# A two-layer encoder whose MLP runs by seven block products: activation sums move into the up product, weight sums move to VectorE, and the first two groups go product by product

## The chip, the cores and the metric

The kernel runs on one core of one Trainium2 chip. The metric is device time: microseconds from start to end of one execution, as a median over runs. The profile is one further execution, recorded by the hardware profiler.

## The reference

What is computed is a trunk of two layers on 1024 tokens of 1024 features in fp32. Each layer adds an attention part and an MLP to x; a last norm follows. The change touches the MLP alone, whose hidden width is 4096:

```python
for l in range(DEPTH):                       # DEPTH = 2
    ...                                      # four kinds of attention heads
    x = x + mix @ w_out[l]
    h = rms_norm(x, norm2_g[l])
    x = x + jnp.square(jax.nn.relu(h @ w_up[l])) @ w_down[l]
return rms_norm(x, final_norm_g)
```

`rms_norm` divides each token's row by the root of its mean square and multiplies by a gain per feature.

## The kernel before

**Data.** x lies in SBUF as eight tiles of 128 features by 1024 tokens, and every product is transposed: features on partitions, tokens along the row. The trace names the tiles x_7209, x_7244, x_7279, x_7314 (features 0 to 511, tiles 0 to 3) and x_6860, x_6927, x_6987, x_7073 (tiles 4 to 7, which the output projection finishes first).

**A matmul is three.** TensorE multiplies fp32 numbers as pairs of fp32r numbers, a high and a low half, in three passes: high weights by high rows (L211), high weights by low rows (L212), low weights by high rows (L213). So each operand has to be split first. The high half is a copy that ScalarE casts (L186), the low half what is left after the high half is subtracted (L180; L190 where the norm's gain is multiplied in). For activations VectorE makes the low half. For weights GpSimd makes it: `wh` is ScalarE's, `wl` GpSimd's, and each has three buffers. All element-wise two-operand work, sums and low halves alike, goes through the helper `tt`, which is L180 on whatever engine.

**Seven products.** Each of the MLP's two products is done in 2 x 2 blocks by seven block products instead of eight, with sums of activations and sums of weights as operands. For the up product the tokens are cut into two halves (n = 0, 1), the input features into two halves (tiles 0 to 3 and 4 to 7), and the hidden features into pairs of output tiles q and q + 16. A **group** is one such q; there are 16. It loads four weight tiles of 128 x 512, called 11, 12, 21 and 22, sums them into further ones (s1 = 21 + 22, and three subtractions in `combos`, on VectorE, all in tiles called `raw`), and runs seven products on TensorE. A product of a group is a **block** of 12 matmuls of 128 x 512: four tiles of input features by three passes. The seven **operands** of activations, 1 to 7, are the same for all groups: operand 1 is the first token half of features 0 to 511, times the gain, 2 the same of features 512 to 1023, 3 the second token half of features 512 to 1023, and 4 to 7 are differences and sums of these. Each is four pairs of high and low tiles, `near` for operands 1, 2 and 6, `far` for the others. **Product n** is the block with operand n, or by its weights: 11 by operand 1, 12 by operand 2, the 21 sum by 7, 22 by 4, s1 by 5, the 11 sum by 6, the 12 sum by 3.

**From PSUM to DRAM.** The four results of a group (two output tiles by two token halves) come out of PSUM over VectorE (L180 with a PSUM tile u, p or q) and ScalarE (copies at L1218, L1228, L1232). Then VectorE multiplies the positive part by `rb` (L1199), the norm's factor of each token, copied to all partitions. ScalarE squares it (L1201), and it is stored to a DRAM array, `acts`, all four stores issued by SyncE. `rb` is made in the opening: ScalarE squares the eight x tiles, VectorE adds them up (tiles `sq`, 128 x 1024), TensorE sums over partitions (L252), VectorE takes the inverse root (L238 to L242, `rs_r`), TensorE spreads it over all partitions (L288), and VectorE copies it out of PSUM (L283). The text calls the last two the **spread of the norm's rows**.

**The down product.** `acts` is read back 128 x 512 at a time (`act`). The hidden features are cut into four **quarters**, each with seven products of four blocks: 28 blocks a quarter, 112 a layer, the same number as in the up product. Each quarter loads 16 weight tiles and 16 activation tiles. It makes the sums of weights on GpSimd (`raw<-raw`, 16 a quarter) and the sums of activations on VectorE (`act<-act`, 16 a quarter), splits the operands into tiles called `op`, and adds each block's result into x on VectorE as it leaves PSUM (`x<-u`, `x<-p`). After the last quarter of layer 1 the final norm runs for each half of the tokens: `final(0)` stands ahead of the last eight blocks, `final(1)` behind them.

**Stages.** The text cuts each MLP into four stretches: the **opening** (from the last eviction of the output projection to the first product), the **up body** (the 112 blocks of the up product), the **hand-over** (the first 16 blocks of the down product) and the **rest of the down product**.

**What sets the order.** TensorE's order in the MLP is written out by hand (`manual_schedule`): the program's own order. The other engines' order is set by a scheduler that goes by an estimate of times, with priorities by place in the program. Loads and stores stand in SyncE's queue in its order. Before the change all seven operands are made ahead of the first product. Buffers come from pools that open and close: `up` with `prep` for the opening and then `ev` for the results inside it, and `down` after all of them are closed. Two more pools outlive these: one of 16 tiles of 128 x 1024 (`big`, of which `far` and `op` are made) and the weight halves'.

## Time and profile before

| what | value |
|---|---|
| median of 3 runs | 3167.83 us |
| lowest, highest | 3164.23, 3170.88 us |
| the profiled execution | 3169.88 us |
| its span (first to last instruction) | 3168.1 us |
| mean granted TensorE clock | 0.900 |
| before the first MLP's opening | 0 to 848.85 us |
| first MLP | 848.85 to 1572.40 us: 723.55 |
| layer 1 ahead of its MLP's opening | 1572.40 to 2413.65 us: 841.25 |
| second MLP and final norm | 2413.65 to 3168.10 us: 754.45 |

The span is from the first to the last instruction of the profiled execution; the time of an execution holds 1.8 us more. PE is TensorE's matmuls, PEld its weight loads, DVE VectorE, ACT ScalarE, POOL GpSimd, SP SyncE. An arrow `out<-in` gives an instruction's tiles. In a row of waits or of idle time, what stands behind `<-` is what ended it. The granted clock is a share of full speed. Line numbers are those of the kernel before.

### The profile page before, as it was taken

Reading aid. Unit: us, or ns where it says so; the run is one execution under the profiler, and the core shown is the slowest. Engines: PE = TensorE matmul, PEld = TensorE weight load, DVE = VectorE, ACT = ScalarE, POOL = GpSimd, SP = SyncE. Lnnn points to the kernel's source line nnn. Section 1 sums busy time; section 2 is a strip of 40 time slices with the busy share of each in tenths; the row PEclk is TensorE's granted clock in tenths of the full one; section 3 lists DMA queues with packets and bytes.
Section 4 is the critical chain, followed back from the end, with each engine's and each line's share of the span. In section 5 each row is a group of like instructions: output and inputs, shape, how many; then the busy total and the mean of one; then the engine's idle time right before and its main releaser. Section 6 shows DMA issues by size and latency. Waiting matters only on the chain.

```text
span 3168.1 us, 36820 instructions
## 1 busy us (share of the span) xinstructions
PE 2697.7 (85%) x12310; PEld 2168.3 (68%) x12310; DVE 1970.6 (62%) x3402; ACT 1430.8 (45%) x2525; POOL 1334.0 (42%) x882
## 2 busy tenths in 40 slices
PE   8579996999779996999976789868995999969997
PEld 6357864677568884777864678646884788747775
DVE  6376843576554447888554767446757444488885
ACT  4256743555344443343414567335644444334344
POOL 2254541210224445788523446211111444468882
PEclk9689986799889998999986899868997999979998
DMA  4322464421223324332232225643211233253311
GB/s 161 111 86 94 137 199 144 142 74 58 65 64 107 113 94 153 113 97 83 82 101 92 84 103 160 194 151 100 81 63 43 90 107 112 85 193 96 96 45 53
DMA packets 159045, 334.59 MB, mean 106 GB/s; under 512 B 17848, under 2 KB 24968, under 8 KB 158856
## 3 DMA queue, kind: packets, MB, share of 16 engines
q1 hardware_dynamic: 158856, 332.25, 32.5%
q8 instruction: 97, 1.59, 0.2%
q14 instruction: 92, 0.75, 0.1%
HBM read 233.93 MB, written 98.25 MB: 105 GB/s over the span
## 4 chain that ended last, share of the span: by engine, by line
PE 59%; DMA 16%; DVE 11%; issue 5%; POOL 4%; ACT 2%; SPq 2%; POOLq 0%; DVEq 0%; ACTq 0%
PE u L213 7%; PE u L211 7%; PE u L212 7%; PE mm L211 4%; PE mm L212 4%; PE mm L213 4%; PE p L213 3%; PE p L211 3%; PE p L212 3%; PE sb L778 3%; DMA ws<-in_w_in 3%; PE tr L814 2%; POOL wl L180 2%; POOL raw L180 2%; DMA kb<-both 2%
## 5 line engine op out<-in xcount | busy, mean ns | idle before, releaser
L180 POOL TENSOR_TENSOR wl<-raw,wh 128x512 fp32r<-128x512 f32 x448 | 632.9, 1415 | 637.7 <-ACT wh L186 626.5
L186 ACT ACTIVATE wh<-raw 128x512 fp32r<-128x512 f32 x448 | 280.9, 627 | 583.4 <-PE u L212 306.8
L180 POOL TENSOR_TENSOR wl<-ws,wh 128x512 fp32r<-128x512 f32 (+1 forms) x114 | 149.7, 1316 | 611.6 <-ACT wh L186 581.1
L180 DVE TENSOR_TENSOR op<-act,op 128x512 fp32r<-128x512 f32 x224 | 291.3, 1333 | 31.7 <-ACT op L186 31.5
L180 DVE TENSOR_TENSOR ptl<-tr,pth 128x512 fp32r<-128x512 f32 (+2 forms) x384 | 238.4, 629 | 114.5 <-ACT pth L186 112.8
L186 ACT ACTIVATE pth<-tr 128x512 fp32r<-128x512 f32 (+2 forms) x384 | 205.7, 547 | 184.6 <-PE tr L814 102.4
L783 ACT ACTIVATE p<-p,nm 128x1024 f32<-128x1024 f32 x192 | 219.9, 1146 | 88.9 <-DVE nm L780 85.3
L211 PE MATMUL u<-op,wh 128*128 128x512 f32 x512 | 209.1, 408 | 59.3 <-ACT wh L186 38.0
L778 PE MATMUL sb<-stack 96*128 96x512 f32 x640 | 219.5, 426 | 29.2 <-DVE nm L780 27.8
L180 POOL TENSOR_TENSOR p<-p 128x1024 f32<-128x1024 f32 x64 | 153.3, 2399 | 183.5 <-ACT p L867 167.4
L213 PE MATMUL u<-op,wl 128*128 128x512 f32 x512 | 210.0, 410 | 18.4 <-POOL wl L180 18.2
L180 DVE TENSOR_TENSOR raw<-raw 128x512 f32<-128x512 f32 x128 | 91.0, 714 | 196.0 <-POOL wl L180 167.0
L180 POOL TENSOR_TENSOR raw<-raw 128x512 f32<-128x512 f32 x128 | 212.4, 1671 | 0.5
L212 PE MATMUL u<-op,wh 128*128 128x512 f32 x512 | 208.0, 406 | 1.2 <-DVE op L180 1.0
L211 PE MATMUL mm<-xh,wh 128*128 128x512 f32 x416 | 175.2, 421 | 29.0 <-ACT wh L186 27.6
L186 ACT ACTIVATE op<-act 128x512 fp32r<-128x512 f32 x224 | 139.5, 629 | 90.7 <-DVE act L180 63.5
L802 PE MATMUL pv<-pth,v 128*128 128x256 f32 x512 | 150.2, 307 | 29.6 <-ACT pth L186 16.4
L212 PE MATMUL mm<-xl,wh 128*128 128x512 f32 x416 | 171.4, 412 | 0.0
L213 PE MATMUL mm<-xh,wl 128*128 128x512 f32 x416 | 170.4, 410 | 0.3
L780 DVE CUSTOM_DVE_ANT_0 p<-sb,zero,nm 128x512 f32<-128x512 f32 x192 | 142.5, 743 | 42.7 <-PE sb L778 39.6
L814 PE MATMUL tr<-ident,p 128*128 128x128 f32 x1024 | 161.3, 277 | 3.9 <-DVE ptl L180 2.8
L186 ACT ACTIVATE wh<-ws 128x512 fp32r<-128x512 f32 (+1 forms) x114 | 69.5, 611 | 202.3 <-PE mm L212 93.4
(245 smaller groups left out, 7143.6 us busy)
## 6 DMA issues: line engine op xcount, KB each, us to landing
raw<-in_w_up SPq DMA_DIRECT2D x128, 256.0 KB
raw<-in_w_down SPq DMA_DIRECT2D x128, 256.0 KB
act<-acts SPq DMA_DIRECT2D x128, 256.0 KB
ws<-in_w_in SPq DMA_DIRECT2D x76, 256.0 KB
acts<-u SPq DMA_DIRECT2D x64, 256.0 KB
rz<-drows SPq DMA_DIRECT2D x40, 256.0 KB
acts<-p SPq DMA_DIRECT2D x32, 256.0 KB
acts<-c SPq DMA_DIRECT2D x32, 256.0 KB
```

Of the source, the lines that this page charges most:

```text
L180: (eng or self.nc.vector).tensor_tensor(out=out, in0=a, in1=b, op=op)
L186: nc.scalar.activation(hi, src, AF.Copy)
L211: mm(ps, w[0], x[0][:, sl], start=start, stop=False)
L212: mm(ps, w[0], x[1][:, sl], start=False, stop=False)
L213: mm(ps, w[1], x[0][:, sl], start=False, stop=stop)
L778: self.nc.tensor.matmul(ps, q[:, qt * P:(qt + 1) * P], k[:, sl], start=i == 0, stop=i == len(passes) - 1)
L780: self.nc.vector.tensor_tensor_reduce(out=p[:, sl], in0=ps, in1=self.zero[:, 0:1].bitcast(F).broadcast_to([P, 512]), scale=-scale, scalar= ...
L783: self.nc.scalar.activation(p, p, AF.Exp, bias=nm[:, 1:2], scale=-1.0, accum_out=z)
L802: nc.tensor.matmul(out, v[:, kt], h[:, sl], start=kt == 0, stop=False)
L814: nc.tensor.transpose(t[:, k * 256 + i * P:k * 256 + (i + 1) * P], p[:, (j * 2 + k) * P:(j * 2 + k + 1) * P], self.ident)
```

## The change

**In the up product.** Each group now stores all seven operands that the down product needs instead of four results: `acts` gets the shape [16, 8, 128, 512], operand o of group q in `acts[q, o]`. Three of these (1, 2, 3) are squared results, and their stores are issued by ScalarE, right behind the squares. The other four (5, 6, 7, 4) are differences that VectorE makes in the up product (`t1`, `t2`, `u2`, `n4`, tiles `ev<-ev`), four instructions a group; SyncE issues their stores. In the first two groups the blocks go product by product: as soon as an operand is there, its product runs for both groups, in the order 2, 1, 6, 5, then 7, 4, 3. The norm's squares come in two parts, tiles 4 to 7 ahead of operand 1 in the program, and the spread of the norm's rows stands between product 5 and product 7. From group 2 on product 12 precedes product 11, and products 4 and 3 of a group run during the next group, as before. A weight tile of 12 is loaded first.

**In the down product.** Quarters go 0 to 3, and each takes the groups 4j to 4j + 3 and weights j and j + 4. All seven operands are loaded (28 tiles a quarter for 16), and no sum of activations is made. The 16 sums of weights a quarter go from GpSimd to VectorE, three of the four behind product 12's blocks, the last behind product 7's. The first weights and operand of the first quarter are given a higher priority by 300 places (`AHEAD`), so that the scheduler may put them ahead of the end of the up product. The order of products within a quarter is 1, 2, 6, 7, 4, 5, 3, as before, and `final(0)` moves behind product 5's four blocks, ahead of product 3's.

**Pools.** One pool serves both products of a layer: 24 tiles of 128 x 512 called `near` (operands 1, 2 and 6 of the up product, then the down product's raw weights), 10 called `raw` (the up product's weights, then the activations read back) and 9 called `ev` (results on their way to `acts`; also the final norm's squares). `t`, `v`, `sq` and `far` are tiles of the `big` pool.

**Numbers.** Per layer GpSimd has 64 instructions less and VectorE 64 more in weight sums; the activation sums, 64 a layer, change their place on VectorE; 48 stores and 48 loads of 256 KB are added.

The diff's core:

```diff
@@ -1111,19 +1111,30 @@
-        acts = self.dram.tile([32, P, S], F, tag="acts", bufs=1, name="acts")
-        with tc.manual_schedule(engines={mybir.EngineType.PE}):
-            self.mlp_up(l, acts)
-            self.mlp_down(l, acts)
+        acts = self.dram.tile([16, 8, P, 512], F, tag="acts", bufs=1, name="acts")
+        with tc.manual_schedule(engines={mybir.EngineType.PE}), \
+                tc.tile_pool(name=f"mlp{l}", bufs=1, reuse_waits="tile") as mp:
+            self.mlp_up(l, acts, mp)
+            self.mlp_down(l, acts, mp)
+    def piece(mp, tag, dt=F, name=None):
+        return mp.tile([P, 512], dt, tag=tag, bufs={"near": 24, "raw": 10, "ev": 9}[tag], name=name or tag)
...
@@ mlp_up @@
+            def relu2(v, src, n):
+                nc.vector.scalar_tensor_tensor(out=v, in0=src, scalar=0.0, in1=rb[:, N[n]],
+                                               op0=ALU.max, op1=ALU.mult)
+                nc.scalar.activation(v, v, AF.Square)
+                return v
+            def keep(q, o, v, eng=None):
+                (eng or nc.scalar).dma_start(acts[q, o], v)
...
+            def p4(s):
+                self.block(s.u, s.c["22"], ops[4], start=False)
+                s.b21 = relu2(tmp(), s.u, 0)
+                keep(s.q, 2, s.b21)
+                self.tt(s.u3, s.p, s.u3, ALU.add)
+                relu2(s.u3, s.u3, 1)
+                keep(s.q, 3, s.u3)
+            def p3(s):
+                self.block(s.p, s.c["12"], ops[3], start=False)
+                self.tt(s.u2, s.p, s.u2, ALU.add)
+                relu2(s.u2, s.u2, 1)
+                t1, t2, n4 = tmp(), tmp(), tmp()
+                sub(t1, s.u2, s.p1)
+                keep(s.q, 5, t1, nc.sync)
+                sub(t2, s.u3, t1)
+                keep(s.q, 6, t2, nc.sync)
+                sub(s.u2, s.u3, s.u2)
+                keep(s.q, 7, s.u2, nc.sync)
+                sub(n4, s.b21, t2)
+                keep(s.q, 4, n4, nc.sync)
...
+            first = [group(q) for q in range(2)]
+            ops[2] = [self.rows_split(near(), x(k + 4, 0), gk(k + 4)) for k in range(4)]
+            for s in first:
+                p12(s)
+            acc = self.squares(self.x[4:], self.big, "big", 16)
+            ops[1] = [self.rows_split(near(), x(k, 0), gk(k)) for k in range(4)]
+            for s in first:
+                p11(s)
...
+            ops[6] = [self.rows_split(near(), t[k]) for k in range(4)]
+            for s in first:
+                p6(s)
+            for s in first:
+                p5(s)
+            acc = self.squares(self.x[:4], self.big, "big", 16, acc)
+            self.spread_here(rb, self.rstd_cols(acc, DM, self.ones[:, 0:1]))
...
@@ mlp_down @@
-            for i, j in enumerate((0, 2, 1, 3)):
-                w = lambda m, h: self.raw_weights(mp, d["w_down"][l, m, 2 * j + h], 20)
...
-                    self.tt(s1[m], a21[m], a22[m], ALU.add, nc.gpsimd)
-                    self.tt(a21[m], a11[m], a21[m], ALU.subtract, nc.gpsimd)
-                    self.tt(a11[m], s1[m], a11[m], ALU.subtract, nc.gpsimd)
-                    self.tt(a12[m], a12[m], a11[m], ALU.subtract, nc.gpsimd)
-                for k in range(4):
-                    sub(b11[k], b12[k], b11[k])
...
+                with tc.high_priority(offset=0 if j else self.AHEAD):
+                    a11, t = [w(m, 0) for m in M], raw_op(1)
+                b = [self.rows_split(self.far(), v) for v in t]
+                for m in M:
+                    self.block(u[m], a11[m], b)
                     add(m, 0, u[m])
...
+                for m in M:
+                    ps = self.bank("p")
+                    self.block(ps, a12[m], b)
+                    add(m, 0, ps)
+                    s1.append(self.raw_weights(mp, "near"))
+                    self.tt(s1[m], a21[m], a22[m], ALU.add)
+                    sub(a21[m], a11[m], a21[m])
+                    sub(a11[m], s1[m], a11[m])
...
```

How the instructions stand is shown at three places of layer 0. First VectorE in the opening, before the change, from x's last evictions (`x_7314<-mm,sum`) on. `t` are the differences on which operands 5, 6 and 4 rest, `near` the low halves of operand 1 (x_7209 to x_7314) and operand 2 (x_6860 on).

```order
L180 TENSOR_TENSOR x_7314<-mm,sum 128x512 x2
L180 TENSOR_TENSOR t<-x_7209 128x512
L180 TENSOR_TENSOR t<-x_7244 128x512
L180 TENSOR_TENSOR t<-x_7279 128x512
L180 TENSOR_TENSOR t<-x_7314 128x512
L190 SCALAR_TENSOR_TENSOR near<-x_7209,par,near 128x512
L190 SCALAR_TENSOR_TENSOR near<-x_7244,par,near 128x512
L190 SCALAR_TENSOR_TENSOR near<-x_7279,par,near 128x512
L190 SCALAR_TENSOR_TENSOR near<-x_7314,par,near 128x512
L190 SCALAR_TENSOR_TENSOR near<-x_6860,par,near 128x512
```

Here operand 1 is followed by operand 2. After the change, where `opl` and `oph` are the low and high halves that were called `near`, `far<-t,far` are low halves of operand 5, `t<-x,par,t` are the sums for operand 6, and L181, L191 and L1251 are what L180, L190 and L1176 were:

```order
L181 TENSOR_TENSOR x_7314<-mm,sum 128x512
L1251 SCALAR_TENSOR_TENSOR t<-x_6987,par,t 128x512
L181 TENSOR_TENSOR t<-x_7314 128x512
L191 SCALAR_TENSOR_TENSOR opl<-x_6860,par,oph 128x512
L191 SCALAR_TENSOR_TENSOR opl<-x_6927,par,oph 128x512
L191 SCALAR_TENSOR_TENSOR opl<-x_6987,par,oph 128x512
L181 TENSOR_TENSOR far<-t,far 128x512
L181 TENSOR_TENSOR raw<-raw 128x512
L1251 SCALAR_TENSOR_TENSOR t<-x_7073,par,t 128x512
L181 TENSOR_TENSOR sq<-sq 128x1024
```

The low halves of operand 2 now come first, three of the four subtractions into `t` stand ahead of x's last eviction, and sums for operand 6, low halves of operand 5, weight sums (`raw<-raw`) of the first two groups and the norm's sums (`sq<-sq`) stand between the low halves that the first products need.

Next VectorE in the hand-over, before the change: the last results of group 15 (u_9862, c_9914, u_9861), then the down product's operands (`op<-act,op`) and its first sums into x.

```order
L180 TENSOR_TENSOR u_9862<-p,u_9862 128x512
L1199 SCALAR_TENSOR_TENSOR u_9862<-u_9862,rb 128x512
L1199 SCALAR_TENSOR_TENSOR c_9914<-u,rb 128x512
L180 TENSOR_TENSOR u_9861<-p,u_9861 128x512
L1199 SCALAR_TENSOR_TENSOR u_9861<-u_9861,rb 128x512
L180 TENSOR_TENSOR op<-act,op 128x512 x4
L180 TENSOR_TENSOR x_7209<-u,x_7209 128x512
L180 TENSOR_TENSOR op<-act,op 128x512
L180 TENSOR_TENSOR x_7244<-u,x_7244 128x512
```

After the change, at the same place (`ev` are the results of groups 14 and 15, `far<-act,far` the down product's operands, `raw<-raw` its weight sums):

```order
L181 TENSOR_TENSOR far<-act,far 128x512
L181 TENSOR_TENSOR raw<-raw 128x512
L1181 SCALAR_TENSOR_TENSOR ev<-u,rb 128x512
L1181 SCALAR_TENSOR_TENSOR ev<-ev,rb 128x512
L181 TENSOR_TENSOR far<-act,far 128x512 x2
L181 TENSOR_TENSOR raw<-raw 128x512
L181 TENSOR_TENSOR far<-act,far 128x512 x2
L181 TENSOR_TENSOR ev<-p,ev 128x512
L181 TENSOR_TENSOR far<-act,far 128x512
L181 TENSOR_TENSOR raw<-raw 128x512
L181 TENSOR_TENSOR far<-act,far 128x512
L1181 SCALAR_TENSOR_TENSOR ev<-ev,rb 128x512
```

The low halves of the down product's operands and its weight sums, of which none stood ahead of group 15's results on VectorE before, are now mixed with these.

Last, ScalarE in the up body, before the change: the casts of weights (`wh<-raw`), the copies out of PSUM and the squares of one group.

```order
L1228 ACTIVATE u_8661<-u 128x512
L186 ACTIVATE wh<-raw 128x512 x2
L1232 ACTIVATE u_8662<-u 128x512
L186 ACTIVATE wh<-raw 128x512
L1201 ACTIVATE u_8662<-u_8662 128x512
L1218 ACTIVATE p_8709<-u 128x512
L186 ACTIVATE wh<-raw 128x512
L1201 ACTIVATE p_8709<-p_8709 128x512
L186 ACTIVATE wh<-raw 128x512
```

After the change, where L1183 is the square, L1208, L1217 and L1198 are the copies and L1187 is the issue of a store:

```order
L1208 ACTIVATE ev<-u 128x512
L187 ACTIVATE wh<-raw 128x512 x2
L1217 ACTIVATE ev<-u 128x512
L187 ACTIVATE wh<-raw 128x512
L1183 ACTIVATE ev<-ev 128x512
L1187 DMA acts<-ev 128x512
L187 ACTIVATE wh<-raw 128x512
L1198 ACTIVATE ev<-u 128x512
L187 ACTIVATE wh<-raw 128x512
```

The issue of a store now stands behind a square in ScalarE's queue, ahead of the next cast of weights; there are three a group.

272 lines of the change are left out of this document (135 added, 137 removed).

## The prediction

> **What bounds the kernel now.** I read the page first: its span and busy times.
>
> ```profile
> span 3168.1 us, 36820 instructions
> PE 2697.7 (85%) x12310; PEld 2168.3 (68%) x12310; DVE 1970.6 (62%) x3402; ACT 1430.8 (45%) x2525; POOL 1334.0 (42%) x882
> ```
>
> TensorE is busy 85% of the time and no other engine comes near, so the question is where the other 15% lies. The two MLPs, cut at TensorE's own edges, answer it for the part that the change touches. The columns are the stretch, its length, the busy time of PE, PEld, DVE, ACT and POOL, the granted clock, the DMA share and GB/s. The rows are opening, up product, hand-over (to the 16th down block) and rest of the down product, for layer 0 and then for layer 1.
>
> ```profile
> 848.75:898.43 49.68, 7.12 (x34) 6.92 (x33) 45.75 (x70) 28.01 (x42) 6.58 (x3) 0.53 0.14 42
> 898.43:1204.50 306.07, 305.38 (x1346) 252.35 (x1345) 137.29 (x169) 125.42 (x220) 141.88 (x109) 1.00 0.31 101
> 1204.50:1289.35 84.85, 54.56 (x194) 41.44 (x193) 67.19 (x63) 29.64 (x50) 52.63 (x34) 0.78 0.54 187
> 1289.35:1572.40 283.05, 270.53 (x1154) 216.88 (x1153) 223.86 (x230) 112.49 (x183) 220.99 (x144) 0.99 0.26 79
> 2413.65:2464.10 50.45, 7.88 (x35) 7.57 (x35) 46.11 (x71) 28.02 (x42) 6.59 (x3) 0.54 0.13 42
> 2464.10:2770.25 306.15, 305.46 (x1344) 252.32 (x1342) 137.44 (x169) 125.44 (x220) 141.60 (x109) 1.00 0.31 101
> 2770.25:2854.70 84.45, 53.53 (x196) 40.27 (x196) 68.38 (x64) 29.99 (x51) 52.88 (x34) 0.78 0.54 189
> 2854.70:3151.04 296.34, 275.25 (x1167) 219.79 (x1165) 238.55 (x259) 124.87 (x205) 218.68 (x142) 0.97 0.22 69
> ```
>
> The up product runs at TensorE's own pace: 112 blocks of 12 matmuls in 306.07 us, 2.73 us a block. By that pace the hand-over's 16 blocks need 43.7 us, so it loses 41.1; the other 96 down blocks need 262.4, so they lose 20.7; the opening has no block and loses 49.7. That is 111.5 us a layer; layer 1 loses 13.3 more in its last stretch, with the final norm. Next, what TensorE waits for there, in its timeline (start, length, engine, line, instruction; in brackets the idle time before it and what ended that):
>
> ```profile
> 895.00 3.78 PE L288 MATMUL mm<-ident,rs_r 128*128 128x128 f32 x16 [4.47 <-DVE rs_r L242]
> 898.43 0.77 PE L211 MATMUL u<-near,wh 128*128 128x512 f32 x1
> ...
> 1198.91 0.50 PE L211 MATMUL u<-far,wh 128*128 128x512 f32 x1 [0.69 <-ACT u L1232]
> 1211.67 0.79 PE L211 MATMUL u<-op,wh 128*128 128x512 f32 x1 [7.03 <-ACT op L186]
> 1257.83 0.79 PE L211 MATMUL u<-op,wh 128*128 128x512 f32 x1 [19.00 <-ACT wh L186]
> ```
>
> In the opening TensorE has no product until VectorE (45.75 of 49.68 us busy) has made all seven operands and the norm's rows. In the hand-over it waits 7 us for the first operand, then 19 us; GpSimd's timeline shows for what, and the waits from 1289 to 1572 (sum, times, longest) that its weight splits limit the rest too.
>
> ```profile
> 1237.84 18.43 POOL L180 TENSOR_TENSOR raw<-raw 128x512 f32<-128x512 f32 x11
> ...
> PE u L213 <- POOL wl L180: 8.7, 10, 2.0
> ```
>
> **The opening.** The prices are in groups by shape (busy us, mean ns; the first three of the opening, the next two of the up body, the last four of the rest of the down product), with the end of x's last eviction:
>
> ```profile
> 848.91 0.69 DVE L180 TENSOR_TENSOR x<-mm,sum 128x512 f32<-128x512 f32 x1 [2.03 <-PE mm L213]
> 849.51 2.49 DVE L180 TENSOR_TENSOR t<-x 128x512 f32<-128x512 f32 x4
> ...
> L180 DVE TENSOR_TENSOR sq<-sq 128x1024 f32<-128x1024 f32 x7 | 8.5, 1214 | 0.5 <-ACT sq L352 0.5
> L190 DVE SCALAR_TENSOR_TENSOR far<-x,par,far 128x512 fp32r<-128x512 f32 x4 | 2.9, 742 | 0.0
> L180 DVE TENSOR_TENSOR far<-t,far 128x512 fp32r<-128x512 f32 x8 | 5.1, 677 | 0.0
> ...
> L180 DVE TENSOR_TENSOR raw<-raw 128x512 f32<-128x512 f32 x49 | 34.9, 712 | 81.8 <-POOL wl L180 69.0 <-DMA raw<-in_w_up 12.4
> L180 POOL TENSOR_TENSOR wl<-raw,wh 128x512 fp32r<-128x512 f32 x88 | 114.3, 1299 | 125.5 <-ACT wh L186 125.5
> ...
> L180 DVE TENSOR_TENSOR op<-act,op 128x512 fp32r<-128x512 f32 x84 | 109.6, 1337 | 7.8 <-ACT op L186 7.8
> L180 DVE TENSOR_TENSOR x<-u,x 128x512 f32<-128x512 f32 x53 | 35.4, 680 | 27.2 <-PE u L213 27.2
> L180 POOL TENSOR_TENSOR wl<-raw,wh 128x512 fp32r<-128x512 f32 x89 | 135.6, 1527 | 58.0 <-ACT wh L186 57.8
> L180 POOL TENSOR_TENSOR raw<-raw 128x512 f32<-128x512 f32 x48 | 79.1, 1655 | 0.2
> ```
>
> Between x's last eviction (done at 849.6) and the copy of the norm's rows, VectorE has 68 instructions before the change and 63 after. It has three 1024-wide additions less (1.21 us each, now made while the output projection runs), two subtractions (0.68) and two fused instructions (0.74) less, and two additions out of PSUM (0.68) more: 5.1 us less. So the spread of the norm's rows, at 895.0 now, comes at 889.9. Of the 63, the last low half of operand 2 is the 15th, of operand 1 the 24th, of operand 6 the 30th; by the means above these end at 861, 869 and 873 us. Eight of the 14 blocks of groups 0 and 1 (products 12, 11, 6 and 5, twice) thus run from 861 on, and the four behind operand 6 take 10.9 us and end by 886: VectorE's chain hides them. After the spread and 3.4 us to the next product (as from 895.00 to 898.43), six blocks remain, 16.4 us, and 1 us for a slow start: 910.7. Before, the 14 blocks end at 898.43 + 38.3 = 936.7. Gain **26**. Its ends: 12, if ScalarE (28.01 us busy, its casts now mixed with copies that wait for TensorE) holds VectorE up by half its own time; 29, if the 63 go back to back as the four subtractions do (2.49 us, 0.62 each).
>
> **The up body.** VectorE gets four subtractions a group: 64 a layer at 0.71 to 1.34 us on top of 137.29 of 306, at most 223. The weight sum only moves to a later place in its queue. ScalarE gets three store triggers a group and SyncE four stores; the 48 stores more a layer are 12.6 MB, 41 GB/s on 101. A full stretch of the queues shows what they carry:
>
> ```profile
> 1220.00:1230.00 10.00, 10.00 (x45) 8.26 (x45) 8.78 (x11) 5.55 (x10) 4.21 (x4) 1.00 1.05 387
> ```
>
> So nothing of it reaches TensorE: **0**, at worst a loss of 5 us a layer where results wait for one of nine buffers. What hides the triggers is ScalarE's free time; the third rival takes that cover away.
>
> **The hand-over.** GpSimd's additions go; the first operand is a plain load, issued during the last two groups; and the pool is one, so no load waits for the up product's buffers as a whole. Late next is VectorE. Behind group 14's last eviction, 36 instructions stand in its queue up to the last product of group 15 that ScalarE has yet to square, with the down product's operands and weight sums among them: 33 on SBUF, 3 from PSUM. Call T the end of the last up block. Five blocks lie between, and two waits for ScalarE's copies (0.69 now, 1.9 for both when operand casts stand ahead of them), so the chain starts at T - 14.9. It is 36 x 0.68, and six weight splits of GpSimd at 1.30 that SBUF instructions meet: 32.3, T + 17.4. ScalarE then squares, and casts the down product's fourth weight (1.3): that block starts at T + 18.7 instead of T + 8.2. With 0.8 for its low half and the 1.9, 13 us are lost instead of 41.1. Gain **28**. Ends: 38 (0.62 each and no meeting with GpSimd: 3 lost) and 14 (each of the 33 at 1.337: 27 lost).
>
> **The rest of the down product.** GpSimd's 16 additions a quarter (1.655) go: its 28 splits at 1.30 to 1.53 fill 36 to 43 us of a quarter's 76.5. VectorE loses 16 subtractions and gets 16 additions: no change. SyncE has 28 operand loads a quarter for 16, at 41 GB/s on 79. Loss 3 instead of 20.7: gain **18**; ends 21 and 9 (12 lost if VectorE's load, 223.86 of 283.05, holds TensorE up). The final norm of the first half now stands behind four more blocks. Of its gap in layer 1,
>
> ```profile
> 3121.28 1.86 PE L252 MATMUL u<-ones,sq 128*128 128x1 f32 x8 [5.64 <-DVE sq L180]
> 3125.38 2.08 PE L288 MATMUL u<-ident,rs_r 128*128 128x128 f32 x8 [2.23 <-DVE rs_r L242]
> ```
>
> the 5.64 are covered, and some of the slow clock behind it: gain **8** (0 to 12), once.
>
> **Sum.** (26 + 28 + 18) x 2 + 8 = 152. The profiled execution took 3169.88 us, 1.8 over its span and 2.05 over the median of the three runs: 3169.9 - 152 = 3018, less 2: **3016**. All good ends give 188, 2980; all bad (12 + 14 + 9 - 5) x 2 = 60, 3108.
>
> **Rivals.** *VectorE takes GpSimd's place as the limit.* For it: two of its instructions, one of which meets a split of GpSimd, take 2.38 us.
>
> ```profile
> 1300.77 2.38 DVE L180 TENSOR_TENSOR op<-act,op 128x512 fp32r<-128x512 f32 x2
> ...
> 1300.98 1.62 POOL L180 TENSOR_TENSOR wl<-raw,wh 128x512 fp32r<-128x512 f32 x1 [1.29 <-ACT wh L186]
> ```
>
> If all on SBUF pay the mean of 1.337, a quarter needs 44 x 1.337 + 28 x 0.68 = 78 us against 76.5, the hand-over loses 27 and the rest 12: (26 + 14 + 9) x 2 + 8 = 106, so 3062. Against it: GpSimd's load falls from 221 of 283 us to about 55%. 10%. [...]
>
> *The opening runs at half clock.* The clock is 0.53 in the opening's rows, and the first blocks after the pause at 1211 need 0.43 us a matmul:
>
> ```profile
> 1218.83 0.63 PE L213 MATMUL u<-op,wl 128*128 128x512 f32 x1
> 1219.25 0.63 PE L211 MATMUL u<-op,wh 128*128 128x512 f32 x1
> ```
>
> If pauses for operands keep it there, a block takes 5.1 us: from 861 eight end at 902, and the spread and six more blocks end at 932 to 936. The opening gains 4 instead of 26: 152 - 44 = 108, 3060. Against it: from operand 1 on, blocks follow each other. 9%. [...]
>
> *Slower: ScalarE's triggers hold up the weight casts.* All stores are SyncE's now; three a group come to stand in the queue that casts every weight, into three buffers. SyncE's waits for squared tiles in the up body (sum, times, longest):
>
> ```profile
> SPq L155 <- ACT u L1201: 52.4, 28, 8.4
> ```
>
> ScalarE is busy 7.8 us a group (125.42 / 16) of 19.1. If a trigger holds it for t, TensorE loses 3t - 11.3 a group, 32 times: more than the 152 from t = 5.3 us on. At 6 us it is 214: 3016 + 214 = 3230. Against it: the mean wait is 1.9, and most of that is for a square which on ScalarE stands ahead in its own queue. 5%.
>
> That the loads are not drawn forward is excluded: SyncE's queue has them between the last groups' weights.
>
> **How the numbers follow.** The forecast has 72%, the rivals 10, 9 and 5, and 4 are left for what lies between and no change. The forecast's own ends rarely fall together; 2980 to 3070 takes in the two faster rivals and holds 8 in 10. Faster by over 0.2% (6 us, about what a measurement of this kernel can tell from no change): 0.93; within: 0.02; slower: 0.05.
>
> **What would show it.** Right: TensorE's first products between 853 and 862 us, the spread near 890, blocks at 2.73 us in the up body, no idle time over 10 us in the hand-over, GpSimd without weight additions and under 60% busy in the down product. Wrong: in the up body, idle time of TensorE that ScalarE's casts end (third rival); in the down product, that VectorE ends (first); a clock of 0.5 through the opening (second). A time outside 2980 to 3070 breaks the sum.

## The result, and the profile after

The changed kernel takes 3022.15 us (median of 4 runs, 3021.41 to 3027.09), the kernel before in the same session 3166.03 (4 runs): a ratio of 0.9547, 95% interval 0.953 to 0.9563. The forecast was 3016, range 2980 to 3070. The profiled execution of the changed kernel took 3027.09 us, with this span and these busy times:

```profile
span 3024.9 us, 37460 instructions
PE 2669.2 (88%) x12310; PEld 2163.7 (72%) x12310; DVE 1999.9 (66%) x3530; ACT 1428.3 (47%) x2525; POOL 1125.4 (37%) x754
```

The span is 143.2 us shorter. To see where, both traces are cut at the same blocks of TensorE: from x's last eviction to the start of the 15th block (the first two groups' 14 blocks are then done), to the 105th, to the 129th (the last 8 up blocks and the first 16 down blocks, the hand-over with the end of the up product), and to the end of the down product. First layer 0 of the kernel before (columns as in the prediction):

```profile
849.60:936.94 87.34, 45.52 (x200) 38.81 (x201) 59.68 (x87) 42.01 (x66) 23.37 (x16) 0.73 0.20 63
936.94:1181.74 244.80, 244.80 (x1081) 202.70 (x1080) 115.09 (x143) 101.87 (x179) 117.33 (x90) 1.00 0.33 107
1181.74:1289.35 107.61, 76.63 (x290) 59.20 (x288) 74.77 (x72) 38.34 (x65) 60.38 (x40) 0.83 0.46 161
1289.35:1572.54 283.19, 270.67 (x1154) 217.02 (x1153) 224.00 (x230) 112.63 (x184) 220.99 (x144) 0.99 0.26 79
```

Then layers 0 and 1 of the changed kernel:

```profile
851.67:919.14 67.47, 47.58 (x200) 38.65 (x201) 57.34 (x79) 37.02 (x62) 25.81 (x16) 0.85 0.17 55
919.14:1166.76 247.62, 245.09 (x1081) 202.78 (x1080) 179.94 (x198) 102.85 (x180) 123.77 (x90) 1.00 0.46 154
1166.76:1243.46 76.70, 68.48 (x290) 55.51 (x289) 62.62 (x80) 37.74 (x65) 34.05 (x24) 0.96 0.76 261
1243.46:1504.74 261.28, 261.28 (x1154) 216.55 (x1153) 181.18 (x230) 112.67 (x184) 131.90 (x96) 1.00 0.41 126
2343.94:2413.43 69.49, 50.43 (x201) 40.43 (x201) 57.95 (x79) 37.13 (x62) 27.32 (x16) 0.78 0.16 53
2413.43:2662.66 249.23, 246.69 (x1081) 203.86 (x1080) 173.58 (x198) 102.83 (x180) 122.83 (x90) 0.99 0.47 154
2662.66:2738.89 76.23, 68.11 (x289) 55.31 (x288) 64.07 (x79) 37.84 (x65) 34.86 (x24) 0.96 0.76 262
2738.89:3007.96 269.07, 265.55 (x1169) 219.94 (x1167) 197.27 (x260) 124.60 (x206) 132.18 (x94) 0.99 0.39 115
```

In layer 0 the opening gains 87.34 - 67.47 = 19.9 us, the up body loses 2.8, the hand-over gains 30.9 and the rest of the down product 21.9: there TensorE is now busy for all of its 261.28 us, and 96 blocks take 2.72 us each, the same as the 90 blocks of the up body before (244.80 / 90). In layer 1 the same four give 18.7, -4.4, 30.4 and 22.0, and the final norm 6.0. The attention stages add -2.1 and +2.8; the sum is 143.3.

What TensorE still waits for in layer 0, from its timeline:

```profile
899.29 3.68 PE L289 MATMUL mm<-ident,rs_r 128*128 128x128 f32 x16 [8.87 <-DVE rs_r L243]
927.27 0.50 PE L212 MATMUL u<-oph,wh 128*128 128x512 f32 x1 [2.53 <-ACT ev L1198]
1181.76 0.50 PE L212 MATMUL u<-far,wh 128*128 128x512 f32 x1 [1.24 <-ACT ev L1208]
1186.24 0.50 PE L212 MATMUL u<-far,wh 128*128 128x512 f32 x1 [1.45 <-ACT ev L1217]
1194.83 0.80 PE L212 MATMUL p<-far,wh 128*128 128x512 f32 x1 [5.53 <-DVE ev L181]
```

The spread of the norm's rows still stands late, and all that is left of the hand-over's waits (8.2 us) lies in group 15's last three blocks, ahead of the down product.

### The profile page after: what moved, and what is told of

The parts are those of the page before. It is cut to its first block, busy times and chain, and to the rows that moved or that the text cites. A ratio compares the mean times of both kernels' runs of the same rounds, so it can differ in the third digit from the quotient of the medians.

```text
span 3024.9 us, 37460 instructions
## 1 busy us (share of the span) xinstructions
PE 2669.2 (88%) x12310; PEld 2163.7 (72%) x12310; DVE 1999.9 (66%) x3530; ACT 1428.3 (47%) x2525; POOL 1125.4 (37%) x754
## 4 chain that ended last, share of the span: by engine, by line
PE 66%; DMA 16%; DVE 10%; ACT 3%; issue 3%; SPq 2%; POOL 1%; DVEq 0%; ACTq 0%; POOLq 0%
PE u L212 7%; PE u L213 7%; PE u L214 7%; PE mm L212 5%; PE p L212 4%; PE p L214 4%; PE p L213 4%; PE mm L213 4%; PE mm L214 4%; DMA ws<-in_w_in 3%; PE sb L778 3%; PE tr L814 2%; DMA kb<-both 2%; DMA stack<-qb 2%; SPq L153 2%
## 5 line engine op out<-in xcount | busy, mean ns | idle before, releaser
L181 POOL TENSOR_TENSOR wl<-raw,wh 128x512 fp32r<-128x512 f32 x448 | 630.1, 1408 | 705.6 <-ACT wh L187 682.1
L181 POOL TENSOR_TENSOR wl<-ws,wh 128x512 fp32r<-128x512 f32 (+1 forms) x114 | 150.3, 1321 | 613.6 <-ACT wh L187 583.3
L181 DVE TENSOR_TENSOR ptl<-tr,pth 128x512 fp32r<-128x512 f32 (+2 forms) x384 | 238.4, 629 | 105.6 <-ACT pth L187 103.9
L212 PE MATMUL u<-far,wh 128*128 128x512 f32 x768 | 300.1, 391 | 4.8 <-ACT ev L1217 2.5
L213 PE MATMUL u<-far,wh 128*128 128x512 f32 x768 | 299.3, 390 | 0.0
L214 PE MATMUL u<-far,wl 128*128 128x512 f32 x768 | 299.3, 390 | 0.0
L181 DVE TENSOR_TENSOR raw<-raw 128x512 f32<-128x512 f32 x256 | 207.2, 813 | 97.5 <-POOL wl L181 49.4
L212 PE MATMUL p<-far,wh 128*128 128x512 f32 x640 | 252.2, 394 | 11.5 <-DVE ev L181 11.5
L783 ACT ACTIVATE p<-p,nm 128x1024 f32<-128x1024 f32 x192 | 220.0, 1146 | 87.9 <-DVE nm L780 84.2
L213 PE MATMUL p<-far,wh 128*128 128x512 f32 x640 | 251.4, 393 | 0.0
L214 PE MATMUL p<-far,wl 128*128 128x512 f32 x640 | 251.1, 392 | 0.0
L181 DVE TENSOR_TENSOR far<-act,far 128x512 fp32r<-128x512 f32 x224 | 207.9, 955 | 21.3 <-ACT far L187 21.3
L181 POOL TENSOR_TENSOR p<-p 128x1024 f32<-128x1024 f32 x64 | 153.2, 2397 | 183.9 <-ACT p L867 169.6
L181 DVE TENSOR_TENSOR ev<-ev 128x512 f32<-128x512 f32 x142 | 161.0, 1166 | 22.8 <-ACT ev L1183 17.1
L212 PEld LDWEIGHTS u<-far,wh 128*128 128x128 f32 x768 | 144.6, 188 | 36.3 <-ACT ev L1217 3.3
```

Source lines behind the costliest of these rows:

```text
L181: (eng or self.nc.vector).tensor_tensor(out=out, in0=a, in1=b, op=op)
L212: mm(ps, w[0], x[0][:, sl], start=start, stop=False)
L213: mm(ps, w[0], x[1][:, sl], start=False, stop=False)
L214: mm(ps, w[1], x[0][:, sl], start=False, stop=stop)
L783: self.nc.scalar.activation(p, p, AF.Exp, bias=nm[:, 1:2], scale=-1.0, accum_out=z)
```

## The experiments

Each run was cut at the same blocks. The table gives, for layers 0 and 1, the length of the opening from x's last eviction to the 15th block, and the time lost against 2.72 us a block in the three stretches behind it, all from the starts of blocks in TensorE's timeline; then the ratio to the kernel before.

| kernel | opening | up body | hand-over | rest | ratio (95%) |
|---|---|---|---|---|---|
| before | 87.3 / 88.2 | 0 / 0 | 42.3 / 41.4 | 21.9 / 22.0 | 1 |
| changed | 67.5 / 69.5 | 2.8 / 4.4 | 11.4 / 11.0 | 0 / 0 | 0.9547 (0.953 to 0.9563) |
| e1 products after all operands | 78.6 / 78.9 | 2.8 / 2.8 | 10.8 / 11.1 | 0 / 0 | 0.9608 (0.9587 to 0.9628) |
| e2 weight sums on GpSimd | 67.7 / 68.3 | 4.2 / 4.2 | 16.4 / 16.7 | 4.1 / 4.1 | 0.9656 (0.9632 to 0.968) |
| e3 before, weight sums on VectorE | 87.9 / 88.3 | 0 / 0 | 39.7 / 40.2 | 4.0 / 4.0 | 0.9868 (0.9853 to 0.9884) |
| e4 norm's root earlier | 70.1 / 65.8 | 4.5 / 5.0 | 11.2 / 10.9 | 0 / 0 | 0.9555 (0.9538 to 0.9573) |
| e5 activation sums in down | 69.2 / 67.6 | 1.3 / 1.3 | 20.8 / 20.0 | 0 / 0 | 0.9583 (0.9559 to 0.9606) |
| e6 two pools | 69.3 / 67.4 | 4.5 / 2.9 | 23.6 / 23.5 | 0 / 0 | 0.9634 (0.9615 to 0.9654) |
| e7 all stores on SyncE | 67.6 / 68.2 | 4.1 / 2.7 | 10.4 / 11.0 | 0 / 0 | 0.9552 (0.9526 to 0.9577) |
| e8 operands 6, 7 late | 68.4 / 67.4 | 4.5 / 2.9 | 12.3 / 12.6 | 0 / 0 | 0.9615 (0.9589 to 0.9642) |
| e9 changed, again | 68.9 / 69.4 | 4.5 / 4.4 | 11.1 / 10.7 | 0 / 0 | 0.9531 (0.9516 to 0.9546) |
| e10 opening's low halves on VectorE | 67.4 / 65.8 | 4.2 / 4.2 | 10.8 / 11.0 | 0 / 0 | 0.9511 (0.9495 to 0.9526) |
| e11 operands 2, 6 late | 68.9 / 67.5 | 4.5 / 2.9 | 15.0 / 13.5 | 0 / 0 | 0.9598 (0.9576 to 0.9621) |
| e12 e10 and e11 | 67.4 / 66.7 | 4.2 / 4.2 | 15.2 / 12.4 | 0 / 0 | 0.9513 (0.9495 to 0.9531) |

The stages repeat from kernel to kernel within some 2 us where an edit doesn't touch them. The whole time repeats less well: layer 0's attention, whose instructions stand in the same order in all fourteen, took from 841.9 to 855.8 us. In layer 1's attention the order is the changed kernel's in e1, e4 and e9 alone; in the others the scheduler changed it along with the edit, and the stretch took from 830.5 (e12) to 854.2 us (e8), where the changed kernel's took 839.2. The kernel before, run beside each set of experiments, took 3160.18 to 3169.15 us. So what an edit costs is read from the MLP's stages; whole times are compared by the ratios.

**e1: the first products after all operands.**

```diff
-            for s in first:
-                p12(s)
...
+            for p in (p12, p11, p6, p5, p7):
+                for s in first:
+                    p(s)
...
```

> The changed kernel, but the blocks of the first two groups stand behind all seven operands and the spread of the norm's rows, as before the change; nothing else differs. Theory: in the changed kernel the spread comes 47.6 us behind x's last eviction and not 40.3, because the early blocks bring GpSimd's weight splits beside VectorE's instructions, which then take 1.4 to 1.8 us instead of 0.68 to 0.75. Then the spread comes here 40 to 42 us behind x's last eviction, hardly an instruction of VectorE takes over 1.3 us in that stretch, and the 14 blocks behind it make the time 25 to 33 us longer than the changed kernel's: about 3050. Rival: VectorE's instructions are long for another reason (ScalarE's casts or the loads beside them): the spread stays at 46 to 48 us and the time is 40 to 45 us longer, about 3064.

In this kernel products 11 and 12 of the first two groups multiply weights that have already been summed, so the numbers differ there; the work is the same. It took 3042.23 us, 20 more than the changed kernel, for the theory's 25 to 33. Here is the stretch from x's last eviction to the spread, first in the changed kernel (columns as above; the last two engines' times before the clock are ScalarE's and GpSimd's, the one before them VectorE's):

```profile
851.67:899.29 47.62, 27.73 (x113) 21.60 (x113) 46.92 (x64) 29.36 (x48) 19.35 (x11) 0.82 0.12 34
```

The same stretch in e1:

```profile
855.80:892.70 36.90, 3.58 (x17) 3.50 (x17) 36.65 (x59) 22.66 (x36) 5.75 (x3) 0.54 0.00 0
```

And in e10, which comes further down:

```profile
849.20:896.30 47.10, 31.83 (x112) 23.20 (x112) 43.51 (x75) 29.55 (x48) 0.00 (x0) 0.83 0.12 34
```

Two groups of VectorE in these stretches (busy us, mean ns), in the changed kernel:

```profile
L191 DVE SCALAR_TENSOR_TENSOR opl<-x,par,oph 128x512 fp32r<-128x512 f32 x8 | 7.8, 998 | 0.1
L1251 DVE SCALAR_TENSOR_TENSOR v<-x,par,v 128x512 f32<-128x512 f32 x4 | 6.0, 1505 | 0.0
```

In e1:

```profile
L191 DVE SCALAR_TENSOR_TENSOR opl<-x,par,oph 128x512 fp32r<-128x512 f32 x8 | 5.8, 749 | 0.1
L1251 DVE SCALAR_TENSOR_TENSOR v<-x,par,v 128x512 f32<-128x512 f32 x4 | 4.0, 998 | 0.0
```

And in e10:

```profile
L191 DVE SCALAR_TENSOR_TENSOR opl<-x,par,oph 128x512 fp32r<-128x512 f32 x8 | 5.9, 744 | 0.1
L1251 DVE SCALAR_TENSOR_TENSOR v<-x,par,v 128x512 f32<-128x512 f32 x4 | 3.0, 740 | 0.0
```

With 3 splits of GpSimd beside it the chain takes 36.9 us, with 11 it takes 47.6; four instructions more of VectorE, of 0.68 us each, account for 2.7 of the difference. What VectorE's groups of 128 x 512 take above the means of e10's stretch, in which GpSimd has nothing to do, is 10.4 us over the 11 splits in the changed kernel (groups `opl<-x` 2.0, `t<-x` 2.5, `v<-x` 3.1, `far<-t` 1.8, `far<-x` 1.0) and 3.1 over the 3 splits in e1: one microsecond for each split, both times. Counted one by one, as many instructions of VectorE of 128 x 512 take over 1 us in these stretches as GpSimd makes splits: 11, 3 and none. The theory's cause holds, though the spread came sooner than its 40 to 42 us. The rival, ScalarE's casts or the loads, would have left 46 to 48 us here; but e1 also has fewer instructions of ScalarE there (x36 for x48) and no transfers, so it's e10 that rules them out: with 48 of ScalarE's and 34 GB/s as in the changed kernel, none of VectorE's is long (the means of its groups of 128 x 512 are 675 to 744 ns). In the changed kernel's down product (layer 0's rest), beside GpSimd's splits, the low halves `far<-act,far` take a mean of 986 ns and the weight sums `raw<-raw` one of 881, both with two inputs in SBUF; the additions `x<-u,x`, with one input in PSUM, keep 684 ns.

**e2: weight sums back on GpSimd.**

```diff
-                    self.tt(s1[m], a21[m], a22[m], ALU.add)
+                    self.tt(s1[m], a21[m], a22[m], ALU.add, nc.gpsimd)
...
```

> The changed kernel with the down product's 16 weight sums a quarter back on GpSimd; pools, operands and order are the changed kernel's. Theory: these sums, at 1.66 us each on GpSimd in front of its splits, made most of both stalls of the kernel before: the rest of the down product loses 15 to 22 us a layer again and the hand-over 10 to 20, so 50 to 85 us longer than the changed kernel: about 3090. Rival: the stalls went because the operands became plain loads in one pool: then at most 15 us longer, about 3030.

It took 3057.92 us: 36 more than the changed kernel, less than the theory's 50 to 85, and more than the rival's 15. The MLP stages hold 19 of these (hand-overs 10.7, rests 8.2), near the rival; layer 1's attention, in another order, took 12 more in the profile. The rest loses 4.1 us a layer, not 15 to 22. GpSimd's timeline tells why. In the kernel before, splits and sums alternated while VectorE had the activation sums as well; they took a mean of 1.515 and 1.655 us in layer 0's rest, and 1.7 us each in this stretch, beside activation sums that took 3.48 us for two and 2.88 for the next two (VectorE's timeline, then GpSimd's):

```profile
1404.53 3.48 DVE L180 TENSOR_TENSOR act<-act 128x512 f32<-128x512 f32 x2
...
1408.53 2.88 DVE L180 TENSOR_TENSOR act<-act 128x512 f32<-128x512 f32 x2
...
1405.73 1.73 POOL L180 TENSOR_TENSOR wl<-raw,wh 128x512 fp32r<-128x512 f32 x1
1407.42 1.75 POOL L180 TENSOR_TENSOR raw<-raw 128x512 f32<-128x512 f32 x1
1409.12 1.74 POOL L180 TENSOR_TENSOR wl<-raw,wh 128x512 fp32r<-128x512 f32 x1
```

A split and a sum took 3.4 us, more than a block's 2.72. In e2 VectorE has less to do (busy for 175.14 of 264.00 us from 1246 to 1510, for 223.86 of 283.05 in the rest before), and splits and sums take a mean of 1.422 and 1.516 us there, many of them 1.29; GpSimd is busy for 206.18 us in layer 0's rest, for 220.99 before:

```profile
1264.53 1.29 POOL L181 TENSOR_TENSOR wl<-raw,wh 128x512 fp32r<-128x512 f32 x1
1265.78 1.29 POOL L181 TENSOR_TENSOR raw<-raw 128x512 f32<-128x512 f32 x1
1267.03 1.29 POOL L181 TENSOR_TENSOR wl<-raw,wh 128x512 fp32r<-128x512 f32 x1
1268.28 1.74 POOL L181 TENSOR_TENSOR raw<-raw 128x512 f32<-128x512 f32 x1
```

**e3: the kernel before with its weight sums on VectorE.**

```diff
-                    self.tt(s1[m], a21[m], a22[m], ALU.add, nc.gpsimd)
+                    self.tt(s1[m], a21[m], a22[m], ALU.add)
...
```

> The kernel before, with nothing changed but that the down product's 16 weight sums a quarter are VectorE's. Theory: GpSimd's sums made the 19 us wait of the hand-over and most of the rest's 20.7 us, and VectorE, which keeps its 16 activation sums here, has just room for them: the hand-over loses 15 to 20 us instead of 41, the rest 5 to 12 instead of 20.7, 60 to 75 us less than before in all, about 3100. Rival: with both kinds of sums VectorE is the limit of the down product: 20 us less than before at best, 3145 or more.

It took 3124.7 us, 41 less than the kernel before, between theory (60 to 75) and rival (20 at best). The rest loses 4.0 us a layer, as the theory had it (5 to 12) and better; the hand-over stays at 40. Its long wait is hardly shorter, now with a second one behind it:

```profile
1255.02 0.80 PE L211 MATMUL u<-op,wh 128*128 128x512 f32 x1 [16.23 <-ACT wh L186]
1262.63 0.80 PE L213 MATMUL u<-op,wl 128*128 128x512 f32 x1 [6.40 <-POOL wl L180]
```

ScalarE, whose cast ends the first, waits for VectorE in that stretch, for activation sums and then for the weight sums behind them:

```profile
1241.64 0.63 ACT L186 ACTIVATE op<-act 128x512 fp32r<-128x512 f32 x1 [2.98 <-DVE act L180]
1244.65 4.32 ACT L186 ACTIVATE op<-act 128x512 fp32r<-128x512 f32 x8 [2.38 <-DVE act L180]
...
1254.34 0.63 ACT L186 ACTIVATE wh<-raw 128x512 fp32r<-128x512 f32 x1 [2.96 <-DVE raw L180]
```

So with GpSimd free, VectorE's queue ends the wait at nearly the same place. It holds both kinds of sums here, and the run doesn't tell which of them keeps it. The kernel before shows that the wait hung on VectorE there too, in VectorE's and ScalarE's timelines:

```profile
1238.36 5.09 DVE L180 TENSOR_TENSOR act<-act 128x512 f32<-128x512 f32 x3
...
1253.51 3.75 ACT L186 ACTIVATE op<-act 128x512 fp32r<-128x512 f32 x7 [4.38 <-DVE act L180]
1257.16 0.61 ACT L186 ACTIVATE wh<-raw 128x512 fp32r<-128x512 f32 x1
```

The cast of weights that ends the 19 us stands right behind casts of operands, which had waited for activation sums of VectorE, and the three of these above took 1.7 us each beside GpSimd's run of sums. That run had ended at 1237.84 + 18.43 = 1256.27, 0.9 us ahead of the cast. In the rest, the weight sums' move alone (e3) and the change without it (e2) each leave 4 us of 22. In the hand-over the weight sums' move alone brings 1 to 3 us of the 31, and the change with one of its parts put back (e2, e5, e6) still brings 18 to 26.

**e4: the norm's root earlier.**

```diff
             for s in first:
                 p11(s)
+            acc = self.squares(self.x[:4], self.big, "big", 16, acc)
+            col = self.rstd_cols(acc, DM, self.ones[:, 0:1])
...
-            acc = self.squares(self.x[:4], self.big, "big", 16, acc)
-            self.spread_here(rb, self.rstd_cols(acc, DM, self.ones[:, 0:1]))
+            self.spread_here(rb, col)
```

> The changed kernel, but the norm's last four squares, its sum over partitions and its root stand behind product 11 of the first two groups, ahead of operands 5 and 6, and no longer behind product 5; the spread stays where it is. Theory: TensorE's wait of 8.9 us and more ahead of the spread is one for the norm's root, which stands in VectorE's queue behind the low halves of operands 7, 4 and 3; moved ahead of some of them it lets the last six blocks start 6 to 10 us earlier a layer: 12 to 20 us less than the changed kernel, about 3006. Rival: VectorE's work as a whole is late, the root behind it only the last of it: then the low halves of operands 7, 4 and 3 come later by as much as the root comes earlier, and the time is within 4 us of the changed kernel's, about 3022.

3023.82 us: the rival's answer. In layer 1 the spread came 8 us earlier (40.9 us behind x's last eviction for 48.9), but the 14 blocks ended only 3.7 earlier, with a new wait of 3.4 us for ScalarE's copy of product 7's result; in layer 0 the root stood no earlier and the opening took 2.6 longer. VectorE's work as a whole sets most of the opening, not the place of the root in it.

**e5: activation sums back in the down product.**

```diff
-                t1, t2, n4 = tmp(), tmp(), tmp()
-                sub(t1, s.u2, s.p1)
...
+                keep(s.q, 4, s.u2, nc.sync)
...
+                for k in M:
+                    sub(t[k], b12[k], t[k])
+                op5 = op(t)
...
```

> The changed kernel with the activation sums back in the down product: four stores a group and 16 loads a quarter as before the change, 16 subtractions a quarter on VectorE there; one pool, weight sums on VectorE, early loads and the opening stay as changed. Theory, as the last runs left it: the hand-over's 19 us wait ended with VectorE's chain of activation sums as much as with GpSimd's weight sums, since it stayed at 16 us when the weight sums alone moved; so the hand-over loses 25 to 35 us a layer here, against 11 in the changed kernel, and the rest 3 to 6: 35 to 60 us longer than the changed kernel, about 3070. Rival: one pool and early loads made the hand-over short: it loses under 15 and the time is within 15 us of the changed kernel's.

3030.44 us, 8 more than the changed kernel, as the rival had it (within 15) and not the theory (35 to 60). The hand-over loses 20 to 21 us, between theory (25 to 35) and rival (under 15), the rest nothing, the up body 1.3 for 2.8 to 4.4. The new waits are those for operand 6's low halves, which stand behind two sums each:

```profile
1225.96 0.79 PE L213 MATMUL u<-far,wh 128*128 128x512 f32 x1 [3.26 <-DVE far L181]
1229.45 0.80 PE L213 MATMUL u<-far,wh 128*128 128x512 f32 x1 [1.83 <-DVE far L181]
```

**e6: two pools.**

```diff
-                tc.tile_pool(name=f"mlp{l}", bufs=1, reuse_waits="tile") as mp:
-            self.mlp_up(l, acts, mp)
-            self.mlp_down(l, acts, mp)
+                ExitStack():
+            with tc.tile_pool(name=f"up{l}", bufs=1, reuse_waits="tile") as mp:
+                self.mlp_up(l, acts, mp)
+            with tc.tile_pool(name=f"down{l}", bufs=1, reuse_waits="tile") as mp:
+                self.mlp_down(l, acts, mp)
```

> The changed kernel, but the down product has a pool of its own, opened after the up product's is closed; sizes and everything else stay. Theory: the first loads of the down product then wait for the last results again, the first product for its operand (7 us before the change), and VectorE's splits stand behind group 15's results: TensorE waits 8 to 14 us ahead of the down product but no longer in group 15's last blocks: 0 to 12 us longer than the changed kernel over both layers, about 3028. Rival: the one pool carries the hand-over's gain: the hand-over loses 25 us or more a layer, and the time is 30 us longer or more.

3045.86 us: the hand-over loses 23.5, twice as much, and the waits in group 15 are gone but for one; in their place TensorE waits for the first operand and later once for VectorE:

```profile
1201.14 0.79 PE L212 MATMUL u<-far,wh 128*128 128x512 f32 x1 [12.36 <-ACT far L187]
...
1242.21 0.47 PE L212 MATMUL u<-far,wh 128*128 128x512 f32 x1 [4.75 <-DVE x L181]
```

The price, 24 us in all, lies between theory (up to 12) and rival (30 or more): one pool carries 12 us a layer of the hand-over's gain. The higher priority for the first loads (`AHEAD`) carries nothing: with 0 in its place every engine's instructions stand in the same order.

**e7: all stores on SyncE.**

```diff
-                (eng or nc.scalar).dma_start(acts[q, o], v)
+                nc.sync.dma_start(acts[q, o], v)
```

> The changed kernel with all seven stores of a group issued by SyncE, none by ScalarE. Theory: a store's issue holds ScalarE for about 0.4 us, so three a group cost nothing while ScalarE is busy under 10 of a group's 19 us: the time is within 5 us of the changed kernel's, 3022. Rival: the issues hold up weight casts behind squares that are not done; then the first blocks of the up body lose their 3 to 5 us no more and the time is 6 to 10 us less. Against both: SyncE's queue, with waits for squared tiles again ahead of weight loads, costs over 10 us.

3019.76 us, within 5 of the changed kernel, as the theory had it. A store's issue on ScalarE in the up body of the changed kernel (0.33 us is the median of its 96, the longest took 1.42):

```profile
1110.86 0.33 ACTq L1187 DMA_DIRECT2D acts<-ev  x1
```

**e8 and e11: the first quarter's operands later.**

```diff
-                        out.append(self.piece(mp, "raw", name="act"))
+                        out.append(self.piece(mp, "ev" if j == 0 and o in (6, 7) else "raw", name="act"))
```

(e11 has `(2, 6)` for `(6, 7)`.)

> The changed kernel, but the first quarter's operands 6 and 7 are read into the nine result buffers, so that their loads and splits can only come once group 15's results have left these; eight splits fewer stand ahead of those results on VectorE, eight casts fewer on ScalarE. Theory: the 11 us that TensorE loses in group 15's last blocks are waits for results that stand behind the down product's splits; eight of these take 8 to 11 us, so the loss falls to 3 to 6 us a layer and the time by 10 to 16 us, to about 3009. Rival: the loss is the price of GpSimd's weight splits or of ScalarE's copies as such: the loss stays at 9 to 12, or comes back in the down product where operands 6 and 7 are then late, and the time is within 4 us of 3022.

> The changed kernel, but the first quarter's operands 2 and 6 are read into the result buffers (in the run before it was 6 and 7, whose splits turned out to stand behind the result that TensorE waits for). Theory: the last long wait of the up product is for a result that stands behind 18 instructions of VectorE, now behind 14, and ScalarE's copies stand behind fewer casts: the loss in group 15's last blocks falls from 11 to 6 or 8 us a layer, 6 to 10 us less in all if operand 2 is in time for the fifth block of the down product. Rival: operand 2 comes late there and gives back what is won: within 4 us of the changed kernel, or longer.

e8 took 3037.3 us, and the loss stayed at 12 us a layer: the theory failed in this form, since operands 6 and 7 stood behind the result that TensorE waits for (the wait is 5.95 us long, 5.98 in e9). The MLP stages hold some 1.5 of the 15 us that e8 takes more than the changed kernel; layer 1's attention, in another order, took 15 more in the profile. In the changed kernel VectorE's timeline shows what stands ahead of it (`ev<-p`), splits and weight sums of the down product, each sum that meets GpSimd at 1.7 us:

```profile
1184.71 0.68 DVE L181 TENSOR_TENSOR far<-act,far 128x512 fp32r<-128x512 f32 x1
1185.31 2.37 DVE L181 TENSOR_TENSOR raw<-raw 128x512 f32<-128x512 f32 x2
...
1188.80 1.28 DVE L181 TENSOR_TENSOR far<-act,far 128x512 fp32r<-128x512 f32 x2
1190.01 1.76 DVE L181 TENSOR_TENSOR raw<-raw 128x512 f32<-128x512 f32 x1
...
1194.10 0.68 DVE L181 TENSOR_TENSOR ev<-p,ev 128x512 f32<-128x512 f32 x1
```

e11 took four of those splits away. The wait for `ev<-p` fell from 5.53 to 2.40 us, so the queue was the cause, and the rival was right about the rest: operand 2 came late and gave more than that back, as e11's timeline of TensorE shows.

```profile
1185.81 0.64 PE L212 MATMUL p<-far,wh 128*128 128x512 f32 x1 [2.40 <-DVE ev L181]
1202.75 0.49 PE L212 MATMUL p<-far,wh 128*128 128x512 f32 x1 [0.75 <-ACT far L187]
...
1215.23 0.50 PE L214 MATMUL p<-far,wl 128*128 128x512 f32 x1 [2.18 <-POOL wl L181]
```

e11 took 3042.74 us, 23 more than e9 on the same chip, of which the two hand-overs are 7. Layer 1's attention, in another order, was 12 us longer in e11's profile than in e9's. Why is open.

**e9, e10, e12: the changed kernel again, and the opening without GpSimd.** In e10 VectorE makes the low halves of the weights of the first 14 blocks:

```diff
-        self.split(wh, wl, raw, eng=self.nc.gpsimd)
+        self.split(wh, wl, raw, eng=self.low)
...
             first = [group(q) for q in range(2)]
+            self.low = nc.vector
...
+            self.low = nc.gpsimd
             held = []
```

> The changed kernel once more, so that the next three can be compared with it on the same chip. Every theory expects 3018 to 3027 us, the stages of the MLPs within 2 us of the first run, and the attention stages of layers 0 and 1 within 8 us: these differed that much between runs of the same instructions.

> The changed kernel, but the low halves of the weights of the first two groups' 14 blocks are made by VectorE; GpSimd has nothing to do in the opening. Theory: each of GpSimd's splits there holds an instruction of VectorE for about 1.07 us, so VectorE gets some 12 splits of 0.61 us ahead of the spread but loses the collisions: no instruction of 128 x 512 over 1 us, the spread 43 to 45 us behind x's last eviction instead of 47.6, and 6 to 10 us less over both layers than the changed kernel: about 3014. Rival: the long instructions are not GpSimd's doing: the spread comes 53 to 55 us behind the eviction and the time is 10 to 15 us longer, about 3035.

> Both edits of the two runs ahead of this one. Theory: they lie in different stages and add up: 12 to 20 us less than the changed kernel, about 3006. Rival: as for the two by themselves.

e9 took 3019.47 us (3015.69 to 3025.71), e10 3013.85 (3008.89 to 3017.83), e12 3012.73 (3010.43 to 3023.3). In e10 no instruction of VectorE of 128 x 512 takes over 1 us ahead of the spread. VectorE does 11 splits more ahead of the spread (x75 for x64 above) and is still 3.4 us less busy. The spread came 47.1 and 45.9 us behind x's last eviction, not 43 to 45, since VectorE now waits for casts of ScalarE (2.6 us ahead of the 11 splits). The two openings together are 5.1 us shorter than e9's, the medians 5.6 apart. That is less than the theory's 6 to 10 us, and not clear of noise: e10's interval of the ratio (0.9495 to 0.9526) overlaps e9's (0.9516 to 0.9546). The edits did not add up in e12: its hand-overs lose 5.8 us more than e9's, and its time is e10's.

## Why the prediction was right, and where its steps were off

The forecast, 3016 us and 152 us of gain, came out at 3022.15 and 143 to 144, and every gain lay in the stage foreseen for it. That the sum came so close is partly luck: against the forecast the two openings fall short by 13.4 us, the up bodies by 7.2 and the final norm by 2.0, while the hand-overs bring 5.3 and the rests 7.9 more.

- **The opening, 26 foreseen, 19.9 and 18.7 measured.** This is the step that was mis-sized: VectorE's 63 instructions were priced by means of a stretch in which GpSimd made 3 splits (6.58 us busy). The early blocks bring 11 there, eight more, at 1 us each for VectorE (e1, e10): 8 us, where the spread came 47.6 us behind x's last eviction for the 40.3 of the forecast. What follows the spread took 19.9 us, near the forecast's 20.8; the 1 us in it for a slow start, an estimate of the author's, didn't show (the six blocks took 16.4 us, from 902.73 to 919.14). The rival at half clock fell: the granted clock was 0.85 and 0.78 in the opening. ScalarE, from which the lower end of 12 was taken, held VectorE up by 0.3 us (the idle time before `far<-t`). The products' early start is worth 78.6 - 67.5 = 11.1 us in layer 0 (e1); 8.7 come from the rest of the opening, which e1 keeps.
- **The up body, 0 foreseen, 2.8 and 4.4 lost.** Within the 5 allowed. It lies in the second and third block behind the first two groups (2.53 us for ScalarE's copy), not at the store triggers: e7 loses the same without them. An issue took 0.33 us in the median and 1.42 at most, and the rival that needed 5.3 us fell.
- **The hand-over, 28 foreseen, 30.9 and 30.4 measured.** The chain of VectorE was right as a queue and near in size (13 us foreseen to be lost, 11.4 and 11.0 lost), but it stops TensorE four blocks earlier than forecast: in group 15's last product, which waits for VectorE to read PSUM, and not at the down product's fourth weight. The 1.30 us in it for each of six meetings was the mean length of GpSimd's split; no run shows that as VectorE's delay, which in the opening was 1.0 us a split. The reason given for the old wait was half of it. GpSimd's sums ran beside VectorE's activation sums, and the cast that ended the wait came right behind the end of both chains; with the weight sums in VectorE's queue the wait is still 16.23 us (e3). Put back one at a time, weight sums cost 5 to 6 us a layer, activation sums 9, two pools 12 (e2, e5, e6).
- **The rest of the down product, 18 foreseen, 21.9 and 22.0 measured.** Nothing is lost there now, where 3 was allowed. The weight sums alone do give 18 (e3), as the term said; what brings the other 4 is open. A lighter VectorE isn't needed for it: in e5 VectorE is busy for 225.63 of 261.28 us in layer 0's rest and nothing is lost; nor is one pool (e6). In e3 TensorE waits there for ScalarE's operand casts, 1.05 us once a quarter. That VectorE becomes the limit was the first rival; its price shows in the opening instead, and in the down product VectorE is busy 181.18 of 261.28 us, with 986 ns for a mean low half of an operand and not the rival's 1.337 us.
- **The final norm, 8 foreseen, 6.0 measured.** The wait for the squares' sum is gone, and that for the root is now 3.52 us instead of 2.23. Over the 6.4 us from the end of that wait on, the granted clock is 0.62 now (2993.60 to 3000.00) and was 0.53 before (3125.38 to 3131.78). The changed kernel's timeline:

```profile
2993.60 2.08 PE L289 MATMUL u<-ident,rs_r 128*128 128x128 f32 x8 [3.52 <-DVE rs_r L243]
```

## What to carry to other kernels

When an edit starts an engine's work earlier, price its neighbours by the stretch as it will be, with that work in it, and not by their means of before. A long wait names only the chain that ended last: take that chain away on paper, then ask where the next one would end, and whether the work that was moved has made it longer. And where runs of the same instructions differ by more than an edit brings, compare stage by stage, cut at the same blocks.

## What the runs showed of the hardware

In the changed kernel's opening (layer 0), where VectorE was busy for 46.92 of 47.62 us up to the spread, its 128 x 512 instructions took 10.4 us more beside 11 splits of GpSimd than in e10 beside none, and 3.1 us more beside 3 splits in e1 (36.65 of 36.90 us busy): 1.0 us for each split. GpSimd's own instructions of 128 x 512 took 1.73 to 1.75 us beside VectorE's activation sums (the kernel before, 1405.73 to 1410.86), and 1.28 or 1.29 where VectorE was idle or added a PSUM tile (1429.06 to 1432.84). Moving the same work to VectorE (0.68 us an instruction, 11 splits in e10) cost it less than leaving it beside VectorE on GpSimd: 43.51 us busy ahead of the spread for 46.92 in layer 0, 43.50 for 47.52 in layer 1.
